# Gates ahead of attention's end, pooling's first tile between, buffers claimed late: one change to a two-layer hybrid trunk on one Trainium2 core

## The chip, the cores and the metric

The program runs on one core of one Trainium2 chip. The metric is the device time of one execution in microseconds (us). PE is TensorE's matmul path, PEld its weight load, DVE is VectorE, ACT is ScalarE, POOL is GpSimd and SP is SyncE, which here issues every DMA.

## What is computed

Two layers of a gated trunk run over 640 tokens: 128 context tokens and 512 latent tokens, which share one set of weights. Cut to what matters:

```python
h = rmsnorm(x, g_norm) * (1 + scale) + shift
a_u, a_v, b_r, b_k, b_v, b_wd, b_ad, c_q, c_k, c_v, d_p, z, mg = split(h @ w_in)
y_a = chunk_mix(a_u, a_v, w_s, b_s)         # u * (w_s v + b_s), chunks of 128
y_b, s_fin = rwkv7_mix(b_r, b_k, b_v, ...)   # a scan forward and backward
y_c = attention(c_q, c_k, c_v, att_sink)     # windowed, with cached keys
y_d = pool_mix(d_p, pool_w, pool_scale)      # means over 2, 4, 8, 16 tokens
ys = stack([y_a, y_b, y_c, y_d]) * silu(z)
merged = sum(sigmoid(mg) * (ys @ w_up))      # over the four branches
x = x + gate * (merged @ w_o)
```

## The kernel before

Features lie on the partitions and the 640 tokens on the free axis, in two halves of 320. A weight is split into a high and a low part (`whi`, `wlo`) and so is the activation (`hi`, `lo`), and a product is three matmuls of 128x128 by 320 into a PSUM bank tagged `m`. There are four such banks, and one tile of 128 output columns takes two of them (one for each half) and 48 matmuls. These are the *main* matmuls: 7008 of them in the program, walked by the generator `layer` through the list `ORDER`: the inputs of the scan (`k0` to `v1`), the gates of attention (`z20`, `z21`), pooling's tiles (`p0`, `p1`), those of the chunk mixer (`av0`, `av1`, `au0`, `au1`), and then the four merges `0` to `3`, each of eight steps of 60 matmuls. The function `main()` does one such tile.

Beside this stream run generators for what hangs on it: `attention` (with `scores`, `softmax` and `values`, ten blocks of queries), the scan of each half of the heads (`scan`, twice in a layer), pooling (`pool`), the chunk mixer (`mix`), and `modulation_rows`, which makes the second layer's modulation on VectorE, 64 products that are written to `junk`. Small matmuls of these go into the banks `x`, `c` and `o`. A table of latencies and costs in the program (class `Clock`) is stepped as the program is written down and decides after which main matmul each side step is put. On the chip each engine then works through its own list in that order, with semaphores between them.

Around the change the list runs so. `gated(None, "at")` puts the tiles `z20` and `z21` into the four `m` banks and then yields until attention is through (the mark `at`). Only then come, for each of the four halves, a tanh on ACT, the product with `z` on DVE (which reads the bank a last time and so frees it), the product with attention's output `yc`, a copy into `ysh` on ACT and the difference into `ysl` on DVE. Then `x_tile(0)` and `x_tile(1)` (the tags `xm0` and `xm1`, until then attention's inputs and its masks) are claimed for the chunk mixer and for pooling. `pool_mix` and `chunk_v` run twice in turn, in the order `p0`, `av0`, `p1`, `av1`; `chunk_u` multiplies by `au0` and `au1`. The first merge waits for both of pooling's tiles and claims `xm0` and `xm1` for its sums before its first matmul. It takes its first gates and products into `m` banks as well.

In `scores` a block of queries sees one to five blocks of keys of 128 each. All but the first are done in two parts, with a yield between them: each part is written to two `x` banks and read by a reducing instruction on DVE for each head, and a small one takes the larger of the two maxima.

All of these call the engines through one helper (line 290), so rows are told apart by their tiles. `bon` is the scan's bonus term, `qr` and `kb` are its keys and queries, `A` its triangular blocks.

Of the kernel before, what the change touches and what calls it, by code (L numbers as in the profile page):

```python
# [14 lines left out]
P = 128  # L15
# [11 lines left out]

HEAD = ["ck", "cv", "q0", "q1"]
PAIRS = (HEAD[0:2], HEAD[2:4])
ORDER = ["wa", "k0", "v0", "r0", "k1", "r1", "v1", "z20", "z21", "p0", "av0", "p1", "av1", "au0", "au1", 0,  # L30
         "z00", "z01", 1, "z30", "z31", 2, "z10", "z11", 3]
A_TILES = HEAD + [n for n in ORDER if isinstance(n, str)]
A_INDEX = {n: i for i, n in enumerate(A_TILES)}
# [262 lines left out]
def hybrid_layers_kernel(ctx: ExitStack, tc: tile.TileContext, xt, cond, condb, wm, wt, wa, wb, wo, pa, pb, pc, gfin, kctx, vctx,  # L296
# [246 lines left out]
    def modulation_rows():  # L543

        mod_tiles(1)
        sil = S([P, 2, D], "sil")
        dma(sil, condb)
        w = S([P, D], "wt")
        yield "mods0"
        for g in range(2):  # L550
            A.activation(w, sil[:, g], AF.Tanh, scale=0.5)
            V.tensor_scalar(w, w, 1.0, 0.5, ALU.add, ALU.mult)
            V.tensor_tensor(sil[:, g], w, sil[:, g], ALU.mult)
            yield
        for i, (l, kind, n) in enumerate(MOD_ROWS):
            if i:
                w = S([P, D], "wt")
            dma(w, wt[i])
            yield max(ck.after("V", [w], []) - ck.t, 0.0)
            shift, gsc, gt, b1, pr = mods[l]  # L560
            o, width = PRM["bmod"]
            bm = pr[:, o:o + width].rearrange("p (t k) -> p t k", t=3)
            o, width = PRM["gn"]
            gn = pr[:, o:o + width]
            if (l, kind, n) == (1, 1, 0):
                V.tensor_scalar(b1, bm[:, 1], 1.0, None, ALU.add)
            mv = S([P, 2], "mv", 2)
            junk = S([P, D], "junk", dt=mybir.dt.bfloat16)
            for g in range(2):
                while ck.free.get("V", 0.0) > ck.t + 0.3:  # L570
                    yield VQ
                V.tensor_tensor_reduce(junk, w, sil[:, g], 1.0, 0.0, ALU.mult, ALU.add,
                                       mv[:, g:g + 1])
                yield 3.0
            if kind == 0:
                V.tensor_scalar(shift[:, n, :], mv, bm[:, 0, n:n + 1], None, ALU.add)
                ck.mark(f"mod{l}.{n}")
            elif kind == 1:
                V.tensor_scalar(gsc[:, n, :], mv, b1[:, n:n + 1], gn[:, n:n + 1], ALU.add, ALU.mult)
            else:  # L580
                V.tensor_scalar(gt[:, n, :], mv, bm[:, 2, n:n + 1], 0.5, ALU.add, ALU.mult)
            if (kind, n) == (2, KT - 1):
                ck.mark(f"gate{l}")
            if (l, kind, n) == (1, 0, KT - 1):
                ck.mark("mods1")


    def x_tile(b):
        return S([P, KT, HF], f"xm{b}")
# [67 lines left out]
    def layer(l, h, prb):  # L657
# [332 lines left out]
            ck.spawn(f"{L}gn{ft}", group_norm(), 0)  # L990


        def gated(y, need=None):
            hi = S([P, 2, T], "ysh", dt=F32R)
            lo = S([P, 2, T], "ysl", dt=F32R)
            zs = []
            if need:
                for ft in range(2):
                    zs.append((yield from main()))
                yield need  # L1000
                y = inputs["yc"]
            for ft in range(2):
                z = zs[ft] if need else (yield from main())
                for b in range(2):
                    t = S([P, HF], "t", 4)
                    A.activation(t, z[b], AF.Tanh, scale=0.5)
                    V.scalar_tensor_tensor(t, t, 1.0, z[b], ALU.add, ALU.mult)
                    V.scalar_tensor_tensor(t, t, 0.5, y[:, ft, hs[b]], ALU.mult, ALU.mult)
                    A.copy(hi[:, ft, hs[b]], t)
                    V.tensor_tensor(lo[:, ft, hs[b]], t, hi[:, ft, hs[b]], ALU.subtract)  # L1010
            return hi, lo

        mg = []
# [4 lines left out]
                E.tensor_tensor(mhl[b][1][:, k], mg[b][:, k], mhl[b][0][:, k], ALU.subtract)  # L1018

        def merge(i, yhl, mhl):  # L1020
            if i == 0:
                mg.extend(x_tile(b) for b in range(2))
            rhs_y = [((lambda k, b=b: yhl[0][:, k, hs[b]]), (lambda k, b=b: yhl[1][:, k, hs[b]])) for b in range(2)]
            for dt in range(KT):
                gp = [M(), M()]
                yield from accum(gp, piece(), 0, 5, rhs_h, 0, True, False)
                w = piece()
                yield from accum(gp, w, 0, 3, rhs_h, 5, False, True)
                gs = []
                end = i == 3 and dt == KT - 1  # L1030
                if end:
                    mhl.extend((S([P, KT, HF], f"hi{b}", dt=F32R), S([P, KT, HF], f"lo{b}", dt=F32R)) for b in range(2))
                    split_merged(mhl, 0, range(4))
                for b in range(2):
                    g = S([P, HF], "t", 4)
                    A.activation(g, gp[b], AF.Tanh, scale=0.5)
                    gs.append(g)
                    if end and b == 0:
                        split_merged(mhl, 0, range(4, KT - 1), G)
                up = [M(), M()]  # L1040
                yield from accum(up, w, 3, 2, rhs_y, 0, True, True)
                for b, g in enumerate(gs):
                    if i == 0:
                        V.scalar_tensor_tensor(mg[b][:, dt], g, 1.0, up[b], ALU.add, ALU.mult)
                    else:
                        V.scalar_tensor_tensor(g, g, 1.0, up[b], ALU.add, ALU.mult)
                        V.tensor_tensor(mg[b][:, dt], mg[b][:, dt], g, ALU.add)
# [38 lines left out]

        W = 688

        def pool_mix(ft, buf, yd):
            pw = prm("pw").rearrange("p (f c) -> p f c", f=2)  # L1090
            o = yield from main()
            if ft:
                yield f"{L}pool0"
            xp, s2, s4 = (buf[:, i * W:(i + 1) * W] for i in range(3))
            A.copy(xp[:, 16:144], o[0][:, 0:128])
            A.copy(xp[:, 160:352], o[0][:, 128:320])
# [35 lines left out]
        def attention():  # L1132
# [20 lines left out]
            dma(k_o[l], kr[:, 0:TP])  # L1153
            rotate(kr, 0)
            yield f"{L}cv"
            yc = inputs["yc"] = S([P, 2, T], "y", 2)
            pt = S([P, 2 * T], "y", 2)
            vt = inputs["cv"]
            dma(v_o[l], vt[:, 0:TP])
            for t0, n in ((0, 4), (4, 1)):  # L1160
# [21 lines left out]
            def scores():  # L1182
                for i in range(10):
# [13 lines left out]
                    lo = max(qb - 1, 1) if qb else 0  # L1197
                    nl = (qb - lo + 1) * P
                    rs = [slice(0, 64), slice(64, 128)]
                    px = [X(), X()]  # L1200
                    for hh, r in enumerate(rs):
                        mm(px[hh][:, 0:nl], q2[ft][r, qs], kr[r, lo * P:lo * P + nl])
                    for hh in range(2):
                        V.tensor_tensor_reduce(pr[:, hh, 0:nl], px[hh][:, 0:nl], am[:, off:off + nl], 1.0,
                                               -3.0e38, ALU.add, ALU.max, mp[:, 0, hh:hh + 1])
                    if qb:
                        yield
                        m = 384 if qb < 4 else 256
                        px = [X(), X()]
                        for hh, r in enumerate(rs):  # L1210
                            mm(px[hh][:, 0:256], q2[ft][r, qs], kc[r, :])
                        if qb < 4:
                            for hh, r in enumerate(rs):
                                mm(px[hh][:, 256:384], q2[ft][r, qs], kr[r, (qb + 1) * P:(qb + 2) * P])
                        for hh in range(2):
                            V.tensor_tensor_reduce(pr[:, hh, nl:nl + m], px[hh][:, 0:m], am[:, off + nl:off + nl + m], 1.0,
                                                   -3.0e38, ALU.add, ALU.max, mp[:, 1, hh:hh + 1])
                    n = len(blocks) * P
                    mx = mp[:, 0]
                    if qb:  # L1220
                        V.tensor_tensor(mx, mx, mp[:, 1], ALU.max)
                    V.scalar_tensor_tensor(mx, mx, -0.125, nsk[:, f2], ALU.mult, ALU.min)
                    es = S([P, 2], "es", 4)
# [151 lines left out]
        for n, t in (("k0", ta[:, 0]), ("v0", vt), ("r0", ta[:, 2]), ("k1", kx[:, 0]), ("r1", kx[:, 1]), ("v1", kx[:, 2])):  # L1375
            yield from main_to(t)
            ck.mark(L + n)
        g2 = yield from gated(None, f"{L}at")
        ya = S([P, 2, T], "y", 2)
        yd = S([P, 2, T], "y", 2)  # L1380
        tm, buf = x_tile(0).rearrange("p k f -> p (k f)"), x_tile(1).rearrange("p k f -> p (k f)")
        dma(tm[:, 3 * T:3 * T + 512], pc[l][:, 0:512])
        bs = buf[:, 3 * W:3 * W + 256]
        dma(bs, pc[l][:, 512:768])
        dma(buf[:, 3 * W + 256:3 * W + 322], pedge)
        G.memset(buf[:, 0:W], 0.0)
        G.memset(buf[:, W:W + 1], 0.0)
        for ft in range(2):
            yield from pool_mix(ft, buf, yd)
            yield from chunk_v(ft, tm, bs, ya)  # L1390
        yield from chunk_u(ya)
        for ft in range(2):
            yield f"{L}pool{ft}"
        yield from merge(0, g2, mhl)
        g0 = yield from gated(ya)
        yield from merge(1, g0, mhl)
# [247 lines left out]
```

## Time and profile before

| | |
|---|---|
| median of three runs | 1417.62 us (1411.64 to 1418.31) |
| the profiled execution | 1418.08 us, its span 1416.0 us |
| TensorE's mean granted clock in it | 0.991 of full speed |
| PE busy | 1358.9 us, 96% of the span |
| DVE, ACT, POOL busy | 67%, 40%, 4% |
| bytes moved | 132.59 MB, mean 94 GB/s |

A busy PE can be read as busy even where it runs at half its clock or on small tiles; where PE waits, the view of waits names what ended the wait, and the timeline gives its place. The span is counted from the first to the last instruction, and some 2 us lie around it.

### The profile page before, as it was taken

What the parts mean: (1) busy time and instruction counts of PE and PEld (TensorE: products, weight loads), DVE (VectorE), ACT (ScalarE), POOL (GpSimd) and SP (SyncE); (2) the same over time, 40 slices, a digit from 0 to 9 for tenths busy, and PEclk for the clock granted to TensorE, in tenths of its full rate; (3) what the DMA queues carried; (4) which work ended last, traced back from release to release, by engine and by line L of the source; (5) the groups of instructions that cost most, each with busy time, mean ns of one, the idle gap of its engine ahead of it and who ended that gap; (6) DMA issues with size and microseconds to landing.
All of it is one profiled execution on the core that took longest, in us unless ns stands there. A gap on an engine that the chain in (4) does not pass through costs nothing.

```text
span 1416.0 us, 27587 instructions
## 1 busy us (share of the span) xinstructions
PE 1358.9 (96%) x11274; PEld 1256.8 (89%) x11274; DVE 944.7 (67%) x2096; ACT 566.8 (40%) x1252; POOL 50.8 (4%) x43
## 2 busy tenths in 40 slices
PE   6899988999999999999999999999999999999996
PEld 3788878988999988999988888998799999899996
DVE  6666677755876756656887677795466585464476
ACT  5446522235533233324454655223345233232363
POOL 0000010000000000000001000100000000000001
PEclk9999999999999999999999999999999999999998
DMA  9411214421224412562313111424122323144111
GB/s 369 147 53 61 63 40 120 105 82 56 88 65 112 119 55 75 196 234 62 105 61 112 54 46 39 121 79 118 42 59 69 90 81 89 37 128 173 28 38 75
DMA packets 86503, 132.59 MB, mean 94 GB/s; under 512 B 44745, under 2 KB 46153, under 8 KB 84457
## 3 DMA queue, kind: packets, MB, share of 16 engines
q1 hardware_dynamic: 86376, 130.84, 30.1%
q8 instruction: 88, 1.44, 0.4%
q14 instruction: 39, 0.31, 0.1%
HBM read 120.46 MB, written 10.35 MB: 92 GB/s over the span
## 4 chain that ended last, share of the span: by engine, by line
PE 81%; DVE 10%; ACT 4%; issue 2%; DMA 2%; SPq 0%; POOL 0%; DVEq 0%; ACTq 0%; POOLq 0%
PE m L331 63%; PE x L331 10%; PE c L331 4%; PE o L331 2%; DVE wlo L290 2%; DVE t L290 2%; DVE kb L290 2%; ACT whi L290 1%; DMA kb<-ad 1%; PE x L335 1%; DVE nacc L290 1%; PE o L335 1%; DVE lo L290 1%; ACT vn L290 1%; ACT A L290 1%
## 5 line engine op out<-in xcount | busy, mean ns | idle before, releaser
L331 PE MATMUL m<-hi,whi 128*128 128x320 f32 x2064 | 666.7, 323 | 2.9 <-ACT whi L290 1.3
L331 PE MATMUL m<-lo,whi 128*128 128x320 f32 x2064 | 640.8, 310 | 6.0 <-DVE lo L290 5.1
L331 PE MATMUL m<-hi,wlo 128*128 128x320 f32 x2064 | 642.1, 311 | 3.9 <-DVE wlo L290 3.8
L331 PEld LDWEIGHTS m<-hi,whi 128*128 128x128 f32 x2064 | 389.6, 189 | 27.6 <-issue 11.4
L331 PEld LDWEIGHTS m<-lo,whi 128*128 128x128 f32 x2064 | 390.1, 189 | 10.2 <-DVE lo L290 7.1
L331 PEld LDWEIGHTS m<-hi,wlo 128*128 128x128 f32 x2064 | 389.4, 189 | 8.5 <-DVE wlo L290 8.2
L290 ACT CAST whi<-raw 128x640 fp32r<-128x640 f32 (+1 forms) x220 | 148.7, 682 | 296.3 <-PE m L331 270.6
L290 DVE TENSOR_TENSOR wlo<-raw,whi 128x640 fp32r<-128x640 f32 (+1 forms) x220 | 169.2, 772 | 108.6 <-ACT whi L290 105.8
L290 ACT ACTIVATE t<-m 128x320 f32<-128x320 f32 x160 | 68.3, 437 | 88.2 <-PE m L331 88.0
L290 DVE SCALAR_TENSOR_TENSOR t<-t,m 128x320 f32<-128x320 f32 x128 | 61.6, 482 | 58.9 <-PE m L331 43.5
L290 DVE TENSOR_TENSOR kb<-kb 80x31 f32<-80x31 f32 (+15 forms) x248 | 86.1, 347 | 13.0 <-DMA kb<-ad 6.1
L331 PE MATMUL m<-ysh,whi 128*128 128x320 f32 x256 | 84.3, 329 | 1.8 <-DVE t L290 1.6
L290 DVE CUSTOM_DVE_ANT_0 junk<-wt,sil 128x1024 bf16<-128x1024 f32 x64 | 78.4, 1224 | 3.1 <-DMA wt<-wt 3.0
L331 PE MATMUL m<-ysl,whi 128*128 128x320 f32 x256 | 79.6, 311 | 0.0
L331 PE MATMUL m<-ysh,wlo 128*128 128x320 f32 x256 | 79.6, 311 | 0.0
L331 PEld LDWEIGHTS m<-ysh,whi 128*128 128x128 f32 x256 | 48.6, 190 | 5.1 <-DVE t L290 2.1
L290 DVE TENSOR_TENSOR xm<-xm,t 128x320 f32<-128x320 f32 x96 | 48.5, 506 | 3.3
L331 PEld LDWEIGHTS m<-ysl,whi 128*128 128x128 f32 x256 | 48.7, 190 | 0.4
L331 PEld LDWEIGHTS m<-ysh,wlo 128*128 128x128 f32 x256 | 48.6, 190 | 0.0
L290 DVE RECIPROCAL t<-t 128x320 f32<-128x320 f32 x16 | 34.4, 2150 | 19.5 <-ACT t L290 19.5
L290 ACT ACTIVATE vn<-c 64x128 f32<-64x128 f32 x40 | 10.8, 271 | 80.5 <-DVE vn L290 80.5
L290 DVE CUSTOM_DVE_ANT_0 kbt<-x,xm 128x256 f32<-128x256 f32 (+2 forms) x72 | 28.7, 435 | 16.2 <-PE x L331 16.0
(234 smaller groups left out, 1528.4 us busy)
## 6 DMA issues: line engine op xcount, KB each, us to landing
raw<-wb SPq DMA_DIRECT2D x128, 320.0 KB, 3.0
raw<-wa SPq DMA_DIRECT2D x92, 256.0 KB, 2.8
wt<-wt SPq DMA_DIRECT2D x32, 512.0 KB, 3.7
A<-wm SPq DMA_DIRECT2D x4, 1024.0 KB, 9.0
A<-wo SPq DMA_DIRECT2D x8, 512.0 KB, 4.0
xm<-xt SPq DMA_DIRECT2D x4, 640.0 KB
ad<-A SPq DMA_DIRECT2D x8, 320.0 KB, 4.3
qr<-wm SPq DMA_DIRECT2D x2, 1024.0 KB
```

The source lines that it names most:

```text
L290: return f(out, *a, **k)
L331: PE.matmul(out, lhsT, rhs, start=start, stop=stop)
L335: PE.transpose(out, in_, K("ident"))
```

## The change

The list `ORDER` puts `av1` ahead of `p1`, and `layer` follows it. `gates_early` forms tanh and product for `z20` and `z21` at once and keeps the results in the buffer `ysl`; `p0` is computed before attention's end is awaited. After it, pooling's first tile starts (its buffer is claimed and set first), then `gates_late` multiplies the four kept halves by attention's output, in a row, and makes `ysh` and `ysl`. Then come both `chunk_v`, `p1` and pooling's second tile, and `chunk_u`. The first merge no longer waits at its start: it waits for pooling and claims `xm0` and `xm1` after the matmuls of its first step. In `attention` the two buffers `pt` and `yc` are claimed in the other order. In `scores` a block of at most four key blocks is done in one part of up to 512 columns (two of five blocks). The products of `modulation_rows` no longer wait without limit for a free DVE, but yield at most six times. The diff, with the lines that only rename left out:

```diff
-ORDER = [... "z20", "z21", "p0", "av0", "p1", "av1", "au0", "au1", 0,
+ORDER = [... "z20", "z21", "p0", "av0", "av1", "p1", "au0", "au1", 0,
...
-                while ck.free.get("V", 0.0) > ck.t + 0.3:
-                    yield VQ
+                for _ in range(6):
+                    if ck.free.get("V", 0.0) > ck.t + 0.3:
+                        yield VQ
...
-            if need:
-                for ft in range(2):
-                    zs.append((yield from main()))
-                yield need
-                y = inputs["yc"]
...
+        def gates_early():
+            early = S([P, 2, T], "ysl")
+            for ft in range(2):
+                z = yield from main()
+                for b in range(2):
+                    t = early[:, ft, hs[b]]
+                    A.activation(t, z[b], AF.Tanh, scale=0.5)
+                    V.scalar_tensor_tensor(t, t, 1.0, z[b], ALU.add, ALU.mult)
+            return early
+
+        def gates_late(early, y):
+            ts = []
+            for ft in range(2):
+                for b in range(2):
+                    ts.append(S([P, HF], "t", 4))
+                    V.scalar_tensor_tensor(ts[-1], early[:, ft, hs[b]], 0.5, y[:, ft, hs[b]], ALU.mult, ALU.mult)
+            hi = S([P, 2, T], "ysh", dt=F32R)
+            lo = S([P, 2, T], "ysl", dt=F32R)
+            for i, t in enumerate(ts):
+                o = (slice(None), i // 2, hs[i % 2])
+                A.copy(hi[o], t)
+                V.tensor_tensor(lo[o], t, hi[o], ALU.subtract)
+            return hi, lo
...
         def merge(i, yhl, mhl):
-            if i == 0:
-                mg.extend(x_tile(b) for b in range(2))
...
+                if i == 0 and dt == 0:
+                    for ft in range(2):
+                        yield f"{L}pool{ft}"
+                    mg.extend(x_tile(b) for b in range(2))
...
-                    if qb:
-                        yield
-                        m = 384 if qb < 4 else 256
-                        px = [X(), X()]
+                        more = [(kc, 0, 256)] + ([(kr, (qb + 1) * P, P)] if qb < 4 else [])
+                        if len(blocks) <= 4:
+                            parts[0] += more
+                        else:
+                            parts.append(more)
...
-        g2 = yield from gated(None, f"{L}at")
-        ya = S([P, 2, T], "y", 2)
-        yd = S([P, 2, T], "y", 2)
-        tm, buf = x_tile(0).rearrange("p k f -> p (k f)"), x_tile(1).rearrange("p k f -> p (k f)")
+        early = yield from gates_early()
+        p0 = yield from main()
+        yield f"{L}at"
+        buf = x_tile(1).rearrange("p k f -> p (k f)")
...
+        yc = inputs["yc"]
+        yd = S([P, 2, T], "y", 2)
+        pool_mix(0, buf, yd, p0)
+        g2 = gates_late(early, yc)
+        ya = S([P, 2, T], "y", 2)
...
         for ft in range(2):
-            yield from pool_mix(ft, buf, yd)
             yield from chunk_v(ft, tm, bs, ya)
+        p1 = yield from main()
+        yield f"{L}pool0"
+        pool_mix(1, buf, yd, p1)
         yield from chunk_u(ya)
-        for ft in range(2):
-            yield f"{L}pool{ft}"
         yield from merge(0, g2, mhl)
```

What this does to the engines' lists is shown at three places. The first is PE in the first layer, at attention's end. `o<-y` is the last product of attention's values, `x<-bon` a product of the scan, and the rows `m` are main matmuls. Before:

```order
L331 MATMUL m<-hi_210,wlo 128x320
L331 MATMUL o<-y,xm_585 64x128 x8
L331 MATMUL x<-bon,cst 128x320 x2
L331 MATMUL m<-hi_208,whi 128x320
L331 MATMUL m<-lo_209,whi 128x320
```

And with the change, from the product of `bon` on:

```order
L331 MATMUL m<-lo_209,whi 128x320
L331 MATMUL m<-hi_208,wlo 128x320
L331 MATMUL x<-bon,cst 128x320 x2
L331 MATMUL m<-hi_210,whi 128x320
L331 MATMUL m<-lo_211,whi 128x320
```

Before, the product of `bon` stands right behind `o<-y` and ahead of the first main matmul of `p0`. Now 45 main matmuls stand between `o<-y` and it: the last 12 of `z21` and 33 of `p0`.

The second place is PE in the second layer, where `p0` ends. `o<-cst` and `c<-cst` are transposes of attention's probabilities, `c<-y` and `o<-y` products of its values, `x<-qr` products of the scan; the two rows `m` are the last of `p0` and the first of `av0`. With the change:

```order
L331 MATMUL m<-hi_7913,wlo 128x320
L335 MATMUL o<-cst,kbt 128x128 x2
L331 MATMUL x<-bon,cst 128x320 x2
L331 MATMUL c<-y,xm_8124 64x128 x10
L331 MATMUL x<-qr,kb 128x128 x8
L335 MATMUL o<-cst,kbt 128x128 x4
L335 MATMUL c<-cst,kbt 128x128 x4
L331 MATMUL x<-qr,kb 128x128 x8
L331 MATMUL o<-y,xm_8124 64x128 x8
L331 MATMUL x<-qr,kb 128x128 x8
L331 MATMUL m<-hi_7538,whi 128x320
```

Before, in that layer, `o<-y` stands 24 main matmuls ahead of the first of `p0`, the first of these `x<-qr` after six matmuls of `av0`, and 12 or 15 main matmuls between one of them and the next. Now attention's last product stands 72 main matmuls later than before, and three `x<-qr` in a row without a main matmul between.

The third place is DVE at the same point of the second layer. `y<-o` and `y<-c` move attention's transposes out of PSUM, `junk` is a product of the modulation rows, and `A` are the results of `x<-qr` under a mask. With the change:

```order
L290 COPY y<-o 128x256
L290 ISA junk,mv<-wt,sil 128x1024
L290 ISA mv 128x1
L290 TENSOR_TENSOR bon<-x,v 128x320 x2
L290 TENSOR_TENSOR A_9486<-x,cst 128x512
L290 TENSOR_TENSOR A_9487<-x,cst 128x512
L290 ISA junk,mv<-wt,sil 128x1024
L290 ISA mv 128x1
L290 COPY y<-c 128x512
L290 TENSOR_TENSOR A_9486<-x,cst 128x512
L290 TENSOR_TENSOR A_9487<-x,cst 128x512
```

Two `junk`, the product for `bon` and a pair of masked `A` stand between the last two copies of attention's transposes. Before, the same two copies stand so:

```order
L290 COPY y<-o 128x256
L290 TENSOR_TENSOR den<-den,es 128x2
L290 RECIPROCAL den<-den 128x2
L290 TENSOR_SCALAR kbt<-kbt,den 128x512
L290 TENSOR_TENSOR A_8451<-A_8451,A_8243 128x640
L290 TENSOR_TENSOR A_8243<-A_8243 128x640
L290 COPY y<-c 128x512
```

Between them stood attention's own normalization and two products of the scan's keys; with the change these stand ahead of both copies.

## Rows read from the trace of the kernel before

**Rows 1.** The page's part 1: busy time of each engine.

```profile
PE 1358.9 (96%) x11274; PEld 1256.8 (89%) x11274; DVE 944.7 (67%) x2096; ACT 566.8 (40%) x1252; POOL 50.8 (4%) x43
```

**Rows 2.** All waits of PE by releaser: total us, times, longest us.

```profile
PE x L331 <- DVE bon L290: 5.0, 2, 4.0
...
PE x L335 <- DVE A L290: 0.9, 1, 0.9
```

**Rows 3.** Stages of 20 us: busy us of PE, PEld, DVE, ACT, POOL; clock; DMA.

```profile
180.00:200.00 20.00, 15.97 (x114) 14.31 (x113) 15.55 (x27) 6.72 (x18) 1.82 (x3) 0.91 0.13 35
...
480.00:500.00 20.00, 18.58 (x255) 17.45 (x255) 11.20 (x21) 6.32 (x15) 0.00 (x0) 0.79 0.55 146
```

**Rows 4.** PE's timeline, first layer: start, us, instructions, idle time before and releaser.

```profile
187.14 1.71 PE L331 MATMUL x<-bon,cst 128*128 128x320 f32 x4 [4.03 <-DVE bon L290]
...
224.63 0.78 PE L331 MATMUL x<-t,pb 128*128 128x320 f32 x2 [1.77 <-DVE t L290]
...
236.75 0.55 PE L335 MATMUL x<-cst,xm 128*128 128x128 f32 x3 [1.89 <-DVE xm L290]
```

**Rows 5.** The chain of waits, two pieces: start us, us, what.

```profile
188.85 3.22 PE m L331 x13
...
560.85 102.00 PE m L331 x693
```

**Rows 6.** DVE's timeline, first layer at attention's end.

```profile
187.00 0.48 DVE L290 SCALAR_TENSOR_TENSOR t<-t,m 128x320 f32<-128x320 f32 x1
...
188.53 0.49 DVE L290 TENSOR_TENSOR ysl<-t,ysh 128x320 fp32r<-128x320 f32 x1 [0.52 <-ACT ysh L290]
...
194.35 0.49 DVE L290 TENSOR_TENSOR ysl<-t,ysh 128x320 fp32r<-128x320 f32 x1 [0.53 <-ACT ysh L290]
```

**Rows 7.** PE's timeline, second layer around attention's end.

```profile
862.01 1.41 PE L331 MATMUL x<-vn,cst 64*64 64x512 f32 x8 [0.63 <-ACT A L290]
...
874.92 1.34 PE L331 MATMUL x<-bon,cst 128*128 128x320 f32 x4 [1.01 <-DVE bon L290]
...
877.25 0.41 PE L331 MATMUL m<-hi,whi 128*128 128x320 f32 x1 [0.56 <-DVE t L290]
```

**Rows 8.** PE's timeline, single side steps of both layers.

```profile
208.86 1.16 PE L331 MATMUL x<-qr,kb 64*128 64x128 f32 x16
...
864.59 1.31 PE L331 MATMUL c<-y,xm 128*64 128x128 f32 x20
...
867.25 0.60 PE L335 MATMUL c<-cst,kbt 128*128 128x128 f32 x4
...
869.09 1.09 PE L331 MATMUL o<-y,xm 128*64 128x128 f32 x16
```

**Rows 9.** DVE's timeline, second layer, single steps.

```profile
867.96 0.69 DVE L290 COPY y<-c 128x512 f32<-128x512 f32 x1 [1.45 <-PE c L335]
...
871.66 1.54 DVE L290 TENSOR_TENSOR qr<-A,A 128x630 f32<-128x630 f32 x2
...
873.12 0.82 DVE L290 TENSOR_TENSOR bon<-bon,A 128x640 f32<-128x640 f32 x1
...
883.26 0.88 DVE L290 TENSOR_TENSOR bon<-x,v 128x320 f32<-128x320 f32 x2
...
889.60 1.29 DVE L290 TENSOR_TENSOR A<-x,cst 128x512 f32<-128x512 f32 x2 [0.43 <-PE x L331]
...
899.94 1.22 DVE L290 CUSTOM_DVE_ANT_0 junk<-wt,sil 128x1024 bf16<-128x1024 f32 x1
```

**Rows 10.** The chain of waits at two inverses of the scan.

```profile
493.08 1.90 PE m L331 x6
...
494.98 2.27 PE x L331 x80
...
967.09 1.38 PE x L331 x80
```

**Rows 11.** DVE's timeline, one of attention's reductions.

```profile
162.63 0.56 DVE L290 CUSTOM_DVE_ANT_0 kbt<-x,xm 128x384 f32<-128x384 f32 x1 [0.15 <-PE x L331]
```

## What the change should do to the time

> **What bounds the kernel now.** I begin with the page's busy times: PE is busy for 1358.9 us of a span of 1416.0 [rows 1], so every wait of PE in the program adds up to 57 us, and no change that leaves the matmuls alone can give more. The matmuls here stay the same in number. So the question is which waits of PE go, which come, and what TensorE's clock does around them. The view of waits comes next: VectorE's product `bon` makes PE wait 5.0 us in two places, 4.0 of it in one, and its work on `A` 0.9 us [rows 2]. The table of stages then says where time is lost without a wait: in 180 to 200 us and in 480 to 500 us the granted clock is 0.91 and 0.79, a mixture of the levels of 2.4 and 1.2 GHz [rows 3]. The timeline gives the places. In the first layer PE stands for 4.03 us at attention's end, and then twice near pooling, 1.77 us ahead of pooling's second product and 1.89 us inside the chunk mixer's transposes [rows 4].
>
> Why 4 us: all four `m` banks hold `z20` and `z21`, and they are freed only by a product on VectorE that is written down behind the mark `at`. VectorE reaches the first of them at 187.00 us, since it makes the scan's keys and `bon` first, and the product of `bon` on PE stands ahead of `p0` as well [rows 4, 6].
>
> **First layer, attention's end.** `gates_early` frees the banks before the mark, and 45 main matmuls now stand between attention's last product and that of `bon`. A main matmul takes 102.00/693 = 0.147 us [rows 5], so they cover 6.6 us, more than the 4.03 us. The wait goes. With it goes what the clock cost behind it: the four passes of `bon` took 1.71 us where the second layer shows 1.34 [rows 4, 7], 0.37 us, and the next 13 main matmuls 3.22 us where 13 times 0.147 is 1.91 [rows 5], 1.31 us. Sum: 5.7 us.
>
> VectorE gains too. It spent from 187.00 to 194.84 us on the four halves, standing 0.5 us for ACT's copy in each [rows 6]. `gates_late` puts four products and then four differences in a row, 8 times 0.49 = 3.9 us, and the other half of the work is done early. ACT's work is the same.
>
> **First layer, pooling and chunk mixer.** The two waits of 1.77 and 1.89 us come from a `junk` and from an evacuation that came late on VectorE. In the new list 12 and 21 main matmuls (1.8 and 3.1 us) stand between pooling's pairs of products where there were none for the first tile, so these two go: 3.7 us. But the same work now has some 9 us less of PE's time to fit into. Walking down VectorE's new list with these durations I find it behind twice: a `junk` (1.22), an evacuation and a weight split (0.5 and 0.7, an estimate from steps of 320 and 512 columns) and a pair of `A` (1.29) stand together [rows 6, 9] ahead of the banks that the chunk mixer's transposes want, where PE has only six main matmuls and a product to hide them, and pooling's second product of the second tile comes early. I take 1.3 and 0.8 us. Bounds: none, or both waits as before, 3.7. The first layer thus gains 5.7 + 3.7 - 2.1 = 7.3 us, between 5.7 and 9.4.
>
> **Second layer, attention's end.** Here the waits were small: 0.63, 1.01 and 0.56 us [rows 7], and 0.9 us for `A` [rows 2], 3.1 in all. But the new list is worse here. Attention's end comes 72 main matmuls (10.6 us) later in PE's list, behind the end of `p0`, and main work waits for the mark. What PE has there without any main matmul is `bon` (1.34, at its own pace about 0.7), a value product of 1.31 us, three of `x<-qr` at 1.16, two groups of transposes (0.60 each, about 1.0 as they overlap) and the last value product of 1.09 [rows 7, 8]: 7.6 us. VectorE must in the same time finish `qr` (about 1 us of its 1.54 is left), make `bon` (0.82, and a second such step about 0.9), normalize and copy (about 1.2, estimated from the steps of 0.49 and 0.69), a `junk` (1.3 with its reading), `bon<-x` (0.88), a pair of `A` (1.29), a second `junk` (1.3), a copy (0.69) and a second pair of `A` (1.29) [rows 6, 9]: 10.7 us. The first pair of `A` must wait for PE's `x<-qr`, and after the second pair PE has one more `x<-qr` before it is back at main work: 1.0 and 1.16 us. That makes 12.8 us for 7.6 of PE's work, so PE waits 5.2 us. It is not in the trace of before; bounds are nothing, if the list's planner is right about VectorE, and 10.6 us, if all of the later matmuls' length is waited for. My count lies in the middle of these and I keep it.
>
> A stretch of 12.8 us with small matmuls can let the clock fall. After the 4.03 us wait it did, which cost 1.7 us; around 862 to 877 us, with 2.2 us of waits, nothing of that kind shows in the passes of `bon` [rows 4, 5, 7]. I take 1.5 us, between 0 and 7.6 (the side work at half clock throughout).
>
> So the second layer loses 5.2 + 1.5 - 3.1 = 3.6 us, between a gain of 3.1 and a loss of 15.1.
>
> **The scan's small matmuls at 490 us.** There the clock fell: 80 tiny matmuls took 2.27 us where 967 us shows 1.38, and three groups of six main matmuls about 1.90 each in place of 0.88 [rows 3, 10]: 0.89 + 3 times 1.02, or 3.9 us. Before, six main matmuls stood between the two groups there, elsewhere 12 to 18, and there the clock held. Now there are 12 at this place, and 12, 12 and 9 at the others. Since it is a matter of chance where such groups fall, I take half, 2.0 us; bounds: a loss of another 3.9 at a new place, and 3.9 gained.
>
> **Edits that cost nothing.** One part for two of five blocks saves on VectorE, in eight blocks, the fixed share of two reductions and a maximum; a whole reduction of 384 columns takes 0.56 us [rows 11], so it is under 9 us over the program. PE does the same matmuls and VectorE is not the bound elsewhere: hidden under main matmuls; if that cover goes, it is a gain. The limit of six yields moves `junk` without changing how many there are; two of them are in the count above. The later claim of `xm0` and `xm1` lets the first merge step, 60 matmuls or 8.8 us, run beside pooling's second tile; before, PE did not wait at that point, since pooling's last product lay 39 main matmuls ahead in the second layer and 12 in the first. The move of DMAs for the chunk mixer's weights behind `gates_late` leaves them 72 to 78 main matmuls, 11 us, before their first use. On SP they wait for attention's end with the weight loads behind them, which run three pieces (about 10 us) ahead.
>
> **Sum.** 1418.1 - 7.3 + 3.6 - 2.0 = 1412.4, so 1412 us. The profiled execution lies 0.5 us above the median shown, which I neglect; one of three runs lay at 1411.64, so a difference of 0.5% (7 us) is about what a measurement can tell from none. This case alone spans 1407 to 1417.
>
> **Rivals.** *VectorE keeps up.* The planner put `junk` where it saw room; if VectorE is ahead there, the second layer waits for half of my 5.2 us in place of 3.1, the first gains its whole 9.4, and the clock holds at all four inverses: 1418.1 - 9.4 - 0.5 - 3.9 = 1404 us. For it: VectorE is busy for 67% [rows 1]. Against: at attention's end it is at work without a break in both layers.
>
> *VectorE becomes the bound at both ends of attention.* In the first layer the products of the gates come after the scan's keys, behind two `junk`, and the banks stay full: nothing is gained. In the second the whole 10.6 us are waited for, and the clock costs twice the 1.7 us: 1418.1 + 10.6 + 3.4 - 3.1 - 2.0 = 1427 us, slower. It decides from the point where the second layer loses more than the first gains and 7 us over. For it: VectorE has 15.55 us of work in 180 to 200 [rows 3]. Against: in the first layer's list the four early products stand well ahead of the keys.
>
> *The clock stays low in the second layer's whole stretch.* Then the 7.6 us of side work take twice as long, 7.6 us in place of the 1.5 above: 1412.4 - 1.5 + 7.6 = 1418 us, no change. For it: it fell after the 4.03 us wait. Against: it did not around 862 to 877 us [rows 4, 5, 7]. The Trainium skill's page "TensorE: Matmul & The Clock Gate" (Part 1: The HAM clock gate) calls the throttled state the default, which sustained activity releases; read strictly, that rule speaks for this rival and against the change. The trace bears it out at one of two places, so it has a small chance.
>
> *The scan eats the gain.* The scan's last product of the first layer stands 96 main matmuls later than before, so that 96 of 192 (14.1 of 28.2 us) are left ahead of the last gates that want it. If the scan runs another 15 us behind its plan, main work waits for it, and the 7.3 us come back: 1418 us. Against: in the second layer it stands 21 earlier.
>
> **Chances.** The forecast 0.54, VectorE keeping up 0.22, the low clock 0.09, the scan 0.08, VectorE as bound 0.07. Faster by over 0.5% means below 1410.5: nearly all of the second case and a third of the first, 0.39. Slower by over 0.5% is most of the last, 0.06. Between: 0.55. The range, 1403 to 1419, leaves out the last case and the lower tail.
>
> **What would show it.** Right: no wait of PE on `bon` in the first layer, clock 1.0 in 180 to 200 us; in the second layer, between `p0` and `av0`, waits of PE on `A`, `bon` and `y` of about 5 us, with `junk` on VectorE among them. Wrong: a second layer without such a wait, or with a stretch at half clock of more than 5 us; a wait of several us ahead of the fourth merge; a new fall of the clock at an inverse.

## The result, and the profile after

The change makes the kernel faster: 1403.10 us median (1401.68 to 1406.69, 6 runs) beside 1415.14 us (1411.64 to 1418.31, 6 runs), ratio 0.9925 with a 95% interval of 0.9905 to 0.9946. A second measurement gave 1405.18 beside 1412.76 us, 0.9941 [0.9927, 0.9954]. The forecast was 1412 us, with a change of at most 0.5% either way as the likeliest outcome (0.55); the gain is 0.5 to 1.0%. The time lies inside the range of 1403 to 1419, at its very edge, and beside the rival that stood at 1404.

The profiled execution took 1402.3 us. Its page, part 1, and the waits of PE, the rows that answer to [rows 1, 2]:

```profile
span 1400.5 us, 27539 instructions
...
PE 1346.3 (96%) x11274; PEld 1250.7 (89%) x11274; DVE 938.9 (67%) x2056; ACT 566.4 (40%) x1252; POOL 49.9 (4%) x43
```

```profile
PE x L331 <- DVE t L290: 3.2, 3, 1.7
PE x L331 <- DVE bon L290: 2.7, 1, 2.7
...
PE m L331 <- ACT whi L290: 1.8, 1, 1.8
...
PE x L331 <- DVE A L290: 0.6, 1, 0.6
```

The span is 15.5 us shorter, but PE stands only 2.9 us less (1400.5 - 1346.3 = 54.2 us, before 57.1). The other 12.6 us come off PE's busy time, though its matmuls are the same 11274: they ran at a faster pace. Of PE's busy time 6.8 us went ahead of the first main matmul of `wa`, where one execution differs from the next (last section), 5.2 in the third merge, around 490 us, and 3.0 in the first layer around attention's end; elsewhere a little came on. Stages, as in [rows 3], with one of the second layer:

```profile
180.00:200.00 20.00, 20.00 (x163) 18.28 (x161) 17.45 (x33) 5.20 (x12) 1.65 (x1) 1.00 0.24 75
480.00:500.00 20.00, 19.75 (x311) 18.45 (x312) 12.06 (x23) 5.68 (x13) 0.00 (x0) 1.00 0.53 147
...
850.00:870.00 20.00, 17.13 (x161) 13.90 (x162) 17.43 (x35) 6.46 (x18) 0.86 (x3) 1.00 0.20 56
```

The granted clocks of 0.91 and 0.79 of [rows 3] are now 1.00. PE's timeline around attention's end and pooling, for both layers, in place of [rows 4, 7]:

```profile
168.80 1.41 PE L331 MATMUL x<-vn,cst 64*64 64x512 f32 x8 [1.40 <-ACT A L290]
...
200.65 0.83 PE L335 MATMUL x<-cst,xm 128*128 128x128 f32 x5 [0.53 <-DVE A L290]
...
238.02 0.81 PE L331 MATMUL x<-t,pb 128*128 128x320 f32 x2 [0.44 <-DVE t L290]
...
859.97 1.34 PE L331 MATMUL x<-bon,cst 128*128 128x320 f32 x4 [2.67 <-DVE bon L290]
...
867.88 1.75 PE L331 MATMUL x<-qr,kb 64*128 64x128 f32 x16
...
919.73 0.81 PE L331 MATMUL x<-t,pb 128*128 128x320 f32 x2 [1.72 <-DVE t L290]
```

In the first layer 4.03, 1.77 and 1.89 us have become 0.53 and 0.44; ahead of attention's end a wait of 1.40 us on ACT's `A` is new, where before has 0.15. In the second layer, waits of 2.67 and 1.72 us are new.

**Where the time went.** Both kernels start 7008 main matmuls. The start of the same-numbered one in both traces gives the time won (-) or lost (+) in each stretch. The column on the right is against a second profile of the kernel before (below), whose execution took 1411.36 us:

| stretch | against the first profile | against the second |
|---|---|---|
| start, to `z20` | -4.3 | +0.9 |
| first layer's attention stage, `z20` to the first merge's third step | -8.7 | -7.6 |
| on to the end of the first layer | -8.1 | -7.2 |
| second layer's head, its first 192 main matmuls | +2.0 | +2.0 |
| second layer's attention stage, `k0` to the first merge's third step | +2.9 | +2.9 |
| the rest | +0.8 | +0.4 |
| sum | -15.4 | -8.7 |

### The profile page after: what moved, and what is told of

The parts are those of the page before. It is cut to its first block, busy times and chain, and to the rows that moved or that the text cites. A ratio compares the mean times of both kernels' runs of the same rounds, so it can differ in the third digit from the quotient of the medians.

```text
span 1400.5 us, 27539 instructions
## 1 busy us (share of the span) xinstructions
PE 1346.3 (96%) x11274; PEld 1250.7 (89%) x11274; DVE 938.9 (67%) x2056; ACT 566.4 (40%) x1252; POOL 49.9 (4%) x43
## 5 line engine op out<-in xcount | busy, mean ns | idle before, releaser
L290 ACT ACTIVATE t<-m 128x320 f32<-128x320 f32 x152 | 64.8, 437 | 93.3 <-PE m L331 93.1
L290 DVE SCALAR_TENSOR_TENSOR t<-t,m 128x320 f32<-128x320 f32 x120 | 57.7, 481 | 52.9 <-PE m L331 43.4
L290 DVE RECIPROCAL t<-t 128x320 f32<-128x320 f32 x16 | 34.4, 2149 | 18.3 <-ACT t L290 18.3
L290 DVE TENSOR_TENSOR A<-x,cst 128x512 f32<-128x512 f32 x40 | 25.7, 684 | 20.6 <-PE x L331 20.5
```

Source lines behind the costliest of these rows:

```text
L290: return f(out, *a, **k)
```

## The experiments

**The change again.**

> The changed kernel a second time. By the profiled pair, the first main matmul starts 2.1 us earlier and the head of the first layer ends 4.1 us earlier although both kernels do the same work there, and 7.6 us more go where the scan's small matmuls fell to half clock before. Theory 'work': attention's end in the first layer gives 8 to 9 us in every execution (first layer's z20 to the second step of merge 0: 8.7 us shorter than before), the second layer loses 3. Theory 'clock': at least the 4.1 us at the start, and some of the 7.6, are chance of one execution; this profile should then show another start (main matmuls 2 us later) or a fall of the clock at another place, with a time up to 1407. If both gains are the order's, this profile repeats them and the time is 1402 to 1404.

Measured: 1405.18 us (1403.82 to 1406.06). The stretch at 490 us (the 480 main matmuls of the third merge) is again 7.6 us shorter than in the first profile of before, and the second layer's attention stage 3.9 us longer. So these two repeat; the start came out only 1.8 us ahead of before, in place of 4.3. Of the start's difference at least half is chance. In the second layer PE waits 2.67 us on `bon` as in the first profile of the change, but this time the clock falls behind it:

```profile
861.72 1.98 PE L331 MATMUL x<-bon,cst 128*128 128x320 f32 x4 [2.67 <-DVE bon L290]
863.63 2.31 PE L331 MATMUL c<-y,xm 128*64 128x128 f32 x20
```

```profile
860.00:865.00 5.00, 3.28 (x18) 2.20 (x20) 4.63 (x11) 0.72 (x1) 0.00 (x0) 0.73 0.02 7
```

In the first profile of the change these two steps took 1.34 and 1.31 us.

**The gates without the limit and without one-part scores.** The part of the edit that concerns the limit; `scores` goes back to two parts as well:

```diff
-                for _ in range(6):
-                    if ck.free.get("V", 0.0) > ck.t + 0.3:
-                        yield VQ
+                while ck.free.get("V", 0.0) > ck.t + 0.3:
+                    yield VQ
```

> The change without its edit of the scores (blocks in two parts again) and without the limit on the modulation rows. In the program's list the second layer's attention then ends 24 main matmuls ahead of pooling's first tile, as before, and no longer 48 behind its start. Theory 'the gates give, the scores take': the first layer keeps its 8 to 9 us, the second layer no longer loses 3, so 1399 to 1401 us and below the changed kernel. Theory 'the scores give' (a shorter attention is what helps): most of the gain goes, 1409 to 1413 us. Theory 'clock': 1403 to 1411, with the difference at the start and at the scan's small matmuls.

Measured: 1409.99 us, ratio 0.9974 [0.9964, 0.9983]. The first layer's attention stage won 7.1 us against the first profile of before, where the change won 8.7, but the second layer's head lost 8.8 us. The time is the one that the theory "the scores give" named, but by a loss in a place that none of the three theories had. PE's row there, and two of DVE:

```profile
724.00 0.64 PE L331 MATMUL m<-hi,whi 128*128 128x320 f32 x1 [11.23 <-ACT hi L290]
```

```profile
721.39 1.22 DVE L290 CUSTOM_DVE_ANT_0 junk<-wt,sil 128x1024 bf16<-128x1024 f32 x1
722.65 0.23 DVE L290 TENSOR_SCALAR shift<-mv,pa 128x2 f32<-128x2 f32 x1
```

The last `shift` of the second layer's modulation, which every input of that layer needs, is ready at 722.9 us. In the change it was ready at 681.6:

```profile
681.41 0.22 DVE L290 TENSOR_SCALAR shift<-mv,pa 128x2 f32<-128x2 f32 x1
```

**One-part scores in the first layer alone**, the rest of the change as it is:

```diff
-                        if len(blocks) <= 4:
+                        if len(blocks) <= 4 and l == 0:
```

> The changed kernel, with the blocks of four key blocks done in one part in the first layer only; in the second they are in two parts as before. Theory 'the gates give, the scores take': the second layer's attention ends ahead of pooling's first tile again, PE's 5 us of waits there go, and 3 us are gained on the changed kernel: 1399 to 1401 us. Theory 'VectorE keeps up': there was little to gain there, 1402 to 1404.

Measured: 1396.29 us (1394.83 to 1400.63), ratio 0.9884 [0.9866, 0.9901]. The second layer's attention stage is 2.2 us shorter than before instead of 2.9 longer, and the time is lower than the theory had it. PE no longer waits for `bon`:

```profile
863.09 1.24 PE L331 MATMUL x<-bon,cst 128*128 128x320 f32 x4
```

A second measurement was made later:

> The change with the one-part scores in the first layer alone, a second time. Theory (the gain over the change is the 5 us of the second layer's attention stage): 1395 to 1400 us. Rival (the first measurement was low by chance): 1401 to 1405 us, as the change.

It gave 1398.09 us (1396.27 to 1400.15), 0.9889 [0.9850, 0.9928]. This version beats both kernels.

**One-part scores alone, on the kernel before.**

> The kernel before with the edit of the scores alone. Theory 'the scores take': in the second layer attention's last products come 24 main matmuls later, without main matmuls between, so 2 to 5 us slower there; in the first layer attention ends 12 main matmuls earlier but the four banks stay held, so at most 1.8 us are gained. 1415 to 1419 us, against about 1415 for the kernel before. Theory 'the scores give': 1408 to 1411 us.

Measured: 1416.23 us, ratio 1.0032 [1.0016, 1.0048]. The second layer's attention stage lost 11.4 us. PE behind attention's end:

```profile
863.27 0.49 PE L331 MATMUL m<-hi,whi 128*128 128x320 f32 x1 [3.02 <-DVE t L290]
865.21 0.63 PE L331 MATMUL m<-hi,whi 128*128 128x320 f32 x1 [0.92 <-DVE t L290]
```

In the plan this edit alone moves attention's last product of the second layer 24 main matmuls later, behind the gates' tiles, so full `m` banks wait for it again, and the clock fell to 0.83 in 860 to 880 us. By itself the edit is a loss.

**The gates with the limit, scores in two parts in both layers.**

> The change with the block scores left in two parts in both layers; gates, pooling's order, late claim and the limit of six yields stay. Theory (the gates give the first layer 7 to 8.5 us, the limit keeps the second layer's rows in time, the one-part scores are what costs 3 us in the second layer): 1396 to 1400 us, PE's wait of 11 us in the head of the second layer, seen without the limit, is gone, and the second layer's attention stage is 2 to 6 us shorter than in the change. Rival (the early gates themselves make the second layer's modulation late, and the one-part scores make room for it): a wait of PE of more than 5 us stays in the head of the second layer, and the time is 1405 to 1410 us.

Measured: 1400.05 us (1398.70 to 1403.76), 0.9921 [0.9895, 0.9948]. The 11-us wait is gone and the second layer's attention stage is 2.3 us shorter than before. So the one-part scores cost some 5 us there, and the gates cost next to nothing (0.4 us) in the second layer's head once the limit is in.

**The change without the limit**, by the first diff of this section:

> The change with the row step's old wait (as many yields as it takes until VectorE is free by the plan) in place of the limit of six. Theory (the limit is what brings the second layer's shift slab in time): the stop of PE of about 11 us in the head of the second layer comes back with the half clock behind it, and the time is 1408 to 1413 us. Rival (the one-part scores leave VectorE enough room, so the limit has no part in it): no wait of PE over 3 us there, 1401 to 1406 us.

Measured: 1411.71 us, ratio 0.9998 [0.9984, 1.0013]: nothing is left of the gain. PE's wait is even longer than expected, and the clock is low in the stage around its end:

```profile
729.64 0.63 PE L331 MATMUL m<-hi,whi 128*128 128x320 f32 x1 [17.40 <-ACT hi L290]
```

```profile
720.00:740.00 20.00, 10.36 (x50) 10.20 (x51) 12.53 (x26) 4.79 (x10) 0.00 (x0) 0.60 0.35 108
```

DVE shows why: the two last `junk` stand behind a block of the layer's normalization, and the first of them then waits for its weights too.

```profile
720.40 0.55 DVE L290 SCALAR_TENSOR_TENSOR lo<-t,shift,hi 128x320 fp32r<-128x320 f32 x1
...
725.75 1.23 DVE L290 CUSTOM_DVE_ANT_0 junk<-wt,sil 128x1024 bf16<-128x1024 f32 x1 [3.33 <-DMA wt<-wt]
...
728.28 0.23 DVE L290 TENSOR_SCALAR shift<-mv,pa 128x2 f32<-128x2 f32 x1
```

**The limit alone, on the kernel before.**

> The kernel before with the limit of six yields alone. Theory (the old order leaves VectorE free often enough, so the limit matters only beside the early gates): within 3 us of the kernel before, which is 1410 to 1416 us. Rival (the limit is a gain by itself): under 1408 us, with the head of the second layer shorter than before by 3 us or more.

Measured: 1415.86 us, ratio 1.0025 [1.0008, 1.0042]: 2.9 us slower, and not under 1408. But it is no "no effect": against the second profile of before, the two attention stages lost 4.1 and 4.3 us and the stretch at 490 us won 6.5. The theory holds for the sum alone.

**The claim at the merge's start**, the rest of the change as it is:

```diff
         def merge(i, yhl, mhl):
+            if i == 0:
+                for ft in range(2):
+                    yield f"{L}pool{ft}"
+                mg.extend(x_tile(b) for b in range(2))
...
-                if i == 0 and dt == 0:
-                    for ft in range(2):
-                        yield f"{L}pool{ft}"
-                    mg.extend(x_tile(b) for b in range(2))
```

> The change with the first merge's claim of its buffers and its wait for both pooling tiles put back to its start. Theory (PE's matmuls of the first merge step cover the wait for pooling's second tile, which stands only 9 to 12 main matmuls ahead of the merge now): PE waits 1 to 4 us at the first merge in each layer and the time is 1404 to 1409 us. Rival (pooling is done by then, the chunk mixer's products lie between, so the late claim is worth nothing): within 2 us of the change, 1401 to 1406 us, with no wait of PE over 1 us at the first merge.

Measured: 1414.82 us, ratio 1.0022 [1.0009, 1.0035], worse than either theory had it. PE at pooling's second tile, first layer and second, and the stage:

```profile
241.69 1.44 PE L331 MATMUL x<-t,pb 128*128 128x320 f32 x2 [2.25 <-DVE t L290]
...
926.64 1.44 PE L331 MATMUL x<-t,pb 128*128 128x320 f32 x2 [5.39 <-DVE t L290]
...
929.79 1.43 PE L331 MATMUL x<-t,pb 128*128 128x320 f32 x2 [1.72 <-DVE t L290]
```

```profile
920.00:940.00 20.00, 12.89 (x65) 11.30 (x64) 18.15 (x47) 2.18 (x4) 0.48 (x1) 0.74 0.21 54
```

With pooling's second tile behind the chunk mixer's, nothing but the first merge step can cover it. Without that cover the two attention stages are 4.5 and 9.2 us longer than in the change, waits and clock together; some of it comes back later in the second layer.

**The gates behind attention's end**, the rest of the change as it is:

```diff
-        early = yield from gates_early()
+        g2 = yield from gated(None, f"{L}at")
         p0 = yield from main()
-        yield f"{L}at"
...
-        g2 = gates_late(early, yc)
```

> The change with the gates formed as before, behind attention's end; pooling's order, the late claim, the limit of six yields and the one-part scores stay. Theory (the four banks are then full until VectorE comes to the gates, and pooling's first product waits with them): PE waits 4 to 8 us at attention's end in the first layer and about as much more in the second than the change does, and the time is 1408 to 1416 us. Rival (pooling's new order is what gives the gain, and the place of the gates is worth little): 1401 to 1405 us.

Measured: 1417.71 us, ratio 1.0028 [1.0011, 1.0045]. PE's timeline in the first layer and in the second:

```profile
183.84 1.34 PE L331 MATMUL x<-bon,cst 128*128 128x320 f32 x4 [3.18 <-DVE bon L290]
186.18 0.42 PE L331 MATMUL m<-hi,whi 128*128 128x320 f32 x1 [0.56 <-DVE t L290]
192.73 1.62 PE L331 MATMUL x<-qr,kb 64*128 64x128 f32 x16 [1.01 <-DVE bon L290]
...
865.18 0.69 PE L335 MATMUL o<-cst,kbt 128*128 128x128 f32 x2 [3.50 <-DVE y L290]
868.41 2.50 PE L331 MATMUL x<-bon,cst 128*128 128x320 f32 x4 [2.55 <-DVE bon L290]
```

The two attention stages are 5.9 and 6.4 us longer than in the change. So the early gates are worth 12.3 us in these stages; the other edits without them win 1.7 us in the first layer against the second profile of before.

**The kernel before, profiled a second time.**

> The kernel before, unchanged, profiled a second time. Theory (the half clock at 490 us and the late rise of the clock at the start belong to the one profiled execution of before, not to its order of work): the stretch from the start of the third merge to the next product after the inverse (74 main matmuls behind 470 us) is 5 to 8 us shorter than in the first profile, and the time is 1408 to 1414 us. Rival (the order of before, six main matmuls between the small groups there, makes the clock fall every time): the same three slow groups of six at about 1.9 us each, and 1412 to 1418 us.

The time is 1411.36 us, as the theory has it, but for another reason: the rival was right about 490 us. The chain of waits there:

```profile
476.04 4.40 DMA td<-kb
...
480.81 3.06 DMA v<-td
...
483.92 1.45 PE x L331 x78
485.37 1.90 PE m L331 x6
487.26 2.28 PE x L331 x80
489.54 1.90 PE m L331 x6
```

PE's timeline names what came ahead of the fall, 0.59 and 1.01 us on the transfer `v<-td`, which brings the blocks that the inverse multiplies:

```profile
482.70 0.22 PE L331 MATMUL x<-v,A 32*32 32x32 f32 x2 [0.59 <-DMA v<-td]
483.92 1.45 PE L331 MATMUL x<-v,A 32*32 32x32 f32 x78 [1.01 <-DMA v<-td]
```

The first profile of before has the same two waits, 0.59 and 0.82 us. No profile of a changed kernel has them, and none shows the fall. With one-part scores alone, the small groups stand 48 main matmuls earlier and have six main matmuls between them, as before; PE does not wait for the transfer, and the clock holds.

**One step of the scan later, on the kernel before**, to try that cause by itself:

```diff
             dma(s_in, st0[l, :, ft].rearrange("d p v -> p d v"))
             yield
+            if ft and l == 0:
+                yield 3.0
```

> The kernel before with one step put later: in the first layer's second tile of the scan the first small group of the inverse waits 3 us more in the plan, which puts it 21 main matmuls (3.1 us) later on PE. Theory (the half clock at 490 us is set off by PE's wait of 1.4 to 1.6 us on the transfer that this group reads, which both profiles of before show): no wait of PE on that transfer, no half clock, the stretch from the third merge to the product that follows it 6 to 8 us shorter, and 1403 to 1408 us. Rival (the small groups among few main matmuls make the clock fall by themselves): the wait goes, the slow groups of six at about 1.9 us stay, and 1409 to 1413 us.

Measured: 1407.40 us, ratio 0.9979 [0.9964, 0.9994]; the stretch is 6.1 us shorter than in the second profile of before. Neither the wait on the transfer nor the fall is left:

```profile
486.38 1.45 PE L331 MATMUL x<-v,A 32*32 32x32 f32 x80
489.27 1.45 PE L331 MATMUL x<-A,v 32*32 32x32 f32 x80
```

```profile
480.00:500.00 20.00, 18.74 (x339) 17.09 (x340) 10.90 (x25) 6.58 (x20) 0.00 (x0) 1.00 0.46 118
```

The second group still stands behind a few main matmuls of the first (nine in place of six) and takes 1.45 us in place of 2.28. The half clock at 490 us is thus set off by PE's wait on that transfer, and not by the six main matmuls alone.

## Why the prediction was right or wrong

**First layer, attention's end and pooling.** Forecast -7.3 us, measured -7.6 against the second profile of before, -8.7 against the first. The wait of 4.03 us is gone with its slow passes, and the new waits that the walk down DVE's list gave (1.3 and 0.8 us) came as 0.53 and 0.44. That their sum of 2.1 us still comes out is luck: the wait of 1.40 us on `A`, which the forecast did not have, makes up for it. Putting the gates back behind the mark brings a wait of 3.18 us on `bon` again. Apart from the wait on `A` this step was right, place by place.

**Second layer, attention's end.** Forecast +3.6 us, measured +2.9. The new wait is there, on `bon`, of 2.67 us in place of 5.2: behind it PE's side work took 9.7 us (859.97 to the last of the three `x<-qr` at about 869.6), not 7.6, and covered the rest of DVE's list. In this execution the clock cost nothing (1.00 in 850 to 870 us) where 1.5 us was taken; in the second profile of the change it fell behind the same wait, and the stage lost 3.9 us. Further on pooling's second tile waits 1.72 us, which the forecast did not have. So the place and the sign were right, and that the sum is so near is in part luck: the wait was half of what was taken, and another made up for it. Whether the clock costs anything changes from one execution to the next. That the one-part scores in the plan put these two waits there is shown by the kernels that leave them out of this layer: neither wait is in their traces, and the stage is 2.2 and 2.3 us shorter than before.

**The scan at 490 us: a step that failed.** The prediction said that it is "a matter of chance where such groups fall" and took half of 3.9 us. Both profiles of before have the fall, and the change wins 7.1 us there. Two things were mis-read. The price counted four groups, not the others at half clock nor the waits ahead of them. And the cause was taken to be the six main matmuls between small groups; it is a wait of 1.4 us on a transfer, a row of the view of waits of before that was passed over:

```profile
PE x L331 <- DMA v<-td: 1.4, 2, 0.8
```

In the new list the scan's second tile stands 96 main matmuls later, and the transfer is there in time. The prediction had noted that shift, but as a danger ("the scan eats the gain"). No wait of PE on it came.

**The base of the sum.** The opening bound, that all waits of PE add up to 57 us and "no change that leaves the matmuls alone can give more", does not hold: most of the gain in the span came off PE's busy time. The sum was made against an execution of 1418.1 us, "0.5 us above the median shown, which I neglect". That median was of three runs. Later sets of runs of before have medians between 1411.69 and 1412.96 us, and the second profile is 6.7 us shorter, 5.2 of them ahead of the first main matmul of `wa`. By the forecast's own terms (-5.7 us in all) it gives 1405.7 us for the change, against the 1402.3 of its profiled execution. The 3 us that are left are the scan's missing 5.1, less 2.0 us lost in the second layer's head. There PE waits 1.75 us for `whi`, before 0.86, and the clock is 0.91 in 720 to 740 us; nothing in the forecast had this, and no run settles what made `whi` late. Before, and with the change:

```profile
735.59 0.42 PE L331 MATMUL m<-hi,whi 128*128 128x320 f32 x1 [0.86 <-ACT whi L290]
```

```profile
715.32 0.41 PE L331 MATMUL m<-hi,whi 128*128 128x320 f32 x1 [1.75 <-ACT whi L290]
```

So the forecast missed the median by 9 us, mostly by an untypical base and by the scan, and that the time lies inside the range, by 0.1 us, is luck more than foresight.

**Edits that cost nothing.** Here the forecast named the cover, not its worth. The limit of six yields "moves `junk` without changing how many there are": without it the change is 1411.71 us, some 7 to 9 us slower, because the second layer's modulation comes late (its last `shift` at 728.5 us, not 681.6). That it is the early gates which keep DVE busy in the plan is argued, not shown by a run. The late claim "lets the first merge step run beside pooling's second tile": without it 1414.82, some 10 to 12 us slower. The limit alone is a loss on the kernel before (the late claim alone was not tried): inside the change both are conditions for its gain. The one-part scores were hidden in DVE's work, as said, but not their effect on the plan, a loss of 5 us in the second layer's attention stage.

**The rivals.** That VectorE keeps up gave 1404 us, near the time, but not by its way: it had the second layer gain 0.5 us in place of a loss, and it took a first layer of -9.4; only its third term, no fall at the scan's inverses, came. The low clock in the second layer's whole stretch did not come: behind the 2.67 us the granted clock is 1.00 in the first profile of the change, and in the second it fell for a few us only (0.73 in 860 to 865 us, 0.93 in 865 to 870). The prediction took the rule of the Trainium skill's page "TensorE: Matmul & The Clock Gate" (Part 1: The HAM clock gate), that the throttled state is the default and sustained activity releases it, to speak for a fall here; one of the two profiles of the change bears that out, the other does not. VectorE as the bound and the scan as a danger did not come either.

## What to carry to other kernels

Before a stage at half clock is put down to chance, look for the last wait of PE ahead of it, whoever is waited for, and move that step a few matmuls later: 21 main matmuls (3.1 us) gave 6.1 us in that stretch here, and a median 3 to 4 us lower. In a kernel whose order a planner decides, price each small edit by taking it out of the finished change as well as by adding it to the old one: the early gates, the limit and the late claim were worth some 7 to 15 us each inside, each about as much as the whole change gains (8 to 12 us), so their worths do not add up; the limit alone lost 3 us, and the one-part scores were a loss inside too, in the second layer. And make the sum against an execution whose start is typical.

## What was not expected of the hardware

The length of a wait does not decide alone whether the clock falls. Behind 1.4 to 1.6 us at 490 us it fell in both profiles of before. Behind the wait on `bon` in the second layer it stayed at 1.00 in the first profile of the change (2.67 us), and it fell in the second (2.67 us) and in the kernel with the claim at the merge's start (2.68 us, clock 0.91 in 860 to 880 us). What decides between such executions is open.

The start varies between two executions of the same kernel. PE's timeline of before, in its first profile and in its second:

```profile
24.19 1.93 PE L331 MATMUL x<-kb,sc 128*32 128x256 f32 x16
...
30.46 1.94 PE L331 MATMUL x<-A,sc 128*32 128x256 f32 x16
```

```profile
24.55 1.07 PE L331 MATMUL x<-kb,sc 128*32 128x256 f32 x16
...
28.57 1.07 PE L331 MATMUL x<-A,sc 128*32 128x256 f32 x16
```

The same sixteen matmuls take 1.93 or 1.07 us: in the first execution the slow pace lasted until about 34 us, in the second until 24. Both show a granted clock of 1.00 in the stages of 5 us from 15 to 35 us, so this row does not tell the slow start; the durations do. The trace's own records of the clock begin at 34.4 and 24.4 us in these two executions, and the row counts the time ahead of them as full speed. What decides how long the slow start lasts is open.
